# A two-layer diffusion transformer: output projection with latent tokens first, and norm and first up pair by halves of the tokens

## The chip, the cores and the metric

The kernel runs on one core of one Trainium2 chip. The metric is the device time of one execution, in microseconds (us). The core has five engines that work side by side, each with a queue that it follows in order: TensorE (PE, matrix products), VectorE (DVE), ScalarE (ACT), GpSimd (POOL) and SyncE (SP), which only issues loads and stores. They wait for each other by semaphores.

## The reference

Two layers over 512 latent and 256 context tokens of width 1024. Layer 0 mixes tokens by multi-head latent attention, layer 1 by a gated recurrence; each is followed by a SwiGLU feed-forward block of width 2816. The context stream is updated in layer 0 only. The change lies behind the two mixers:

```python
mod_l = jnp.split((jax.nn.silu(c) @ ada_w[i] + ada_b[i])[:, None, :], N_MOD, axis=-1)
mod_c = jnp.split((jax.nn.silu(c_ctx) @ ada_w[i] + ada_b[i])[None, None, :], N_MOD, axis=-1)
...
out_l = merge_heads(o_l) @ w_o
out_c = merge_heads(softmax_attend(q_c, k_c, v_c, scale)) @ w_o
...
x = x + mod_l[2] * o_l
x = x + mod_l[5] * swiglu(modulate(rms_norm(x, norm2_w[i]), mod_l[3], mod_l[4]),
                          ffn_w1[i], ffn_w3[i], ffn_w2[i])
if update_ctx:
    h_ctx = h_ctx + mod_c[2] * o_c
    h_ctx = h_ctx + mod_c[5] * swiglu(modulate(rms_norm(h_ctx, norm2_w[i]), mod_c[3], mod_c[4]),
                                      ffn_w1[i], ffn_w3[i], ffn_w2[i])
```

## The kernel before

**Products.** Activations lie transposed: 128 channels on the partitions, tokens along the free axis. Every fp32 operand is split in two parts, `hi` (a cast to a shorter format, on ScalarE) and `lo` (the rest, a subtraction). Each product is three matmuls, hi·hi, hi·lo and lo·hi (`mm3`, L97 to L99; `mm3m`, L108 to L110, the same for several outputs in turn). A weight block is 128x1024, 512 KB: `weight` loads it into one of four raw buffers (`wf`), ScalarE casts it (`wh`, L83) and GpSimd makes the low part (`wl`, L84), three buffers each. The loads of the modulation weights (`adaw`, in `ada`, L155; products L158, transposes L164) share the four raw buffers.

**Order.** A scheduler of the framework fixes the order of the instructions of each engine ahead of the run, out of the order in which the code issues them, their priorities and the dependences. All loads named here stand in SP's queue.

**Output projection of layer 0.** `w_o` has eight blocks n, one for each 128 output channels. For n = 0 to 2 the product over the 512 latent tokens is computed inside attention, where it fills TensorE's gaps, and stays in three accumulator banks. `mla_out` then goes over n = 0 to 7: the latent product where it is missing (24 matmuls of 128x512), the context product (24 of 128x256) with the same weight, and `residual`, which adds the gated result to x (L557) and the squares to `acc` for the norm. In the rows `oc` and `oa` are the attention results that the products read, `q` is one of five accumulator banks, `L` and `M` are three more.

**Norm.** `norm_rb` makes the reciprocal root of the mean square of each token: transposes of `acc` on TensorE (L205), a reduction on VectorE (L208), a power on GpSimd (L209), a diagonal on VectorE (L212, `dg`), and a product with ones that spreads it over the partitions (L215).

**First up pair.** `ffn` scales x by norm and modulation (L665 on VectorE, L667 on ScalarE) and splits it into operands `op` (L628, L629), for j = 0 to 3 and for two blocks of channels each, over all tokens. The pair needs the tokens as two halves b of hn = 384 (layer 0) or 256 (layer 1) tokens. `strassen_tokens` (L704 to L707, on GpSimd) then makes sums of the quarters for the other ten pairs, which use seven products in place of eight. `ffn_first` computes the first pair directly: for i = 0 and 1 it loads a block of W1 and of W3 and runs four products at once, W1 and W3 for both halves. These are 4 x 48 = 192 matmuls. `ffn_up` does the further pairs, with sums of raw weights (`sa`, `sb`, L611 to L615, on VectorE) and their own casts (`sh`, `sl`, L622, L623).

## Time and profile before

| | |
|---|---|
| time, median of three runs | 1845.55 us (1845.32 to 1850.65) |
| the profiled execution's own time | 1853.65 us |
| its span in the trace | 1851.9 us |
| busy: PE, DVE, ACT, POOL | 1755.5, 1016.3, 762.6, 760.6 us |
| mean granted TensorE clock | 0.982 |
| moved by DMA | 183.61 MB, 99 GB/s on average |

The span runs from the first to the last instruction of one profiled execution; the metric also holds what lies around it. The rows of a timeline give the start of an instruction in us from the span's start, how long it took, the engine, the source line, the operation, the tiles written and read, and in brackets how long the engine stood idle before it and what it waited for. Matmuls overlap each other, so what one of them costs in a dense stretch is the distance between two starts and not its own duration. "x2" is a run of two instructions, with the time of both. The granted clock is a share of TensorE's full 2.4 GHz; its other level is 1.2 GHz.

### The profile page before, as it was taken

The page shows a single profiled execution, that of the slowest core. Times are in us where ns is not written, and L with a number is a line of the kernel's source. Part 1 is how long each engine was busy: PE and PEld are TensorE (multiplying, and loading weights), DVE is VectorE, ACT ScalarE, POOL GpSimd, SP SyncE. Part 2 cuts the span into 40 slices and gives each one's busy share as a digit, 9 for nine tenths or more (in the row PEclk, how much of TensorE's full clock was granted, in tenths as well). Part 3 has the DMA queues.
Part 4 walks back from the last instruction along what each step waited for, and adds up shares of the span by engine and source line. Part 5 has one row for each costly group of instructions (what it writes and reads, how often), then busy time and mean ns, then how long its engine had stood idle before and what let it go on. Part 6 is the DMA issues. An engine that isn't in the chain of part 4 may idle for free. (4 is left out here: it accounts for less than half of the span.)

```text
span 1851.9 us, 33106 instructions
## 1 busy us (share of the span) xinstructions
PE 1755.5 (95%) x13708; PEld 1591.8 (86%) x13708; DVE 1016.3 (55%) x1646; ACT 762.6 (41%) x1467; POOL 760.6 (41%) x528
## 2 busy tenths in 40 slices
PE   4889999999899999999999999999998889999999
PEld 3878989788799999988887888888896779999888
DVE  5567887741754445432203666575745278888400
ACT  4355565532554344432213332423333255555411
POOL 2333342216566666643344554554643440000442
PEclk9999999999999999999999999999999989999999
DMA  7412032523222322254224121111115233333331
GB/s 268 137 39 73 25 116 98 170 74 122 103 86 97 104 96 103 81 168 136 86 71 148 60 69 47 61 55 58 58 35 191 94 137 103 103 115 103 108 118 49
DMA packets 55015, 183.61 MB, mean 99 GB/s; under 512 B 6224, under 2 KB 8528, under 8 KB 54864
## 3 DMA queue, kind: packets, MB, share of 16 engines
q1 hardware_dynamic: 53424, 173.62, 28.5%
q10 hardware_dynamic: 1440, 7.86, 1.2%
q8 instruction: 108, 1.77, 0.4%
q14 instruction: 43, 0.35, 0.1%
HBM read 171.50 MB, written 9.96 MB: 98 GB/s over the span
## 5 line engine op out<-in xcount | busy, mean ns | idle before, releaser
L84 POOL TENSOR_TENSOR wl<-wf,wh 128x1024 fp32r<-128x1024 f32 (+2 forms) x130 | 287.0, 2214 | 438.9 <-ACT wh L83 436.5
L83 ACT CAST wh<-wf 128x1024 fp32r<-128x1024 f32 (+2 forms) x130 | 122.9, 947 | 226.2 <-PE L L98 102.5
L97 PE MATMUL q<-op,sh 128*128 128x384 f32 (+1 forms) x640 | 197.3, 310 | 1.0 <-ACT sh L622 1.0
L98 PE MATMUL q<-op,sh 128*128 128x384 f32 (+1 forms) x640 | 197.6, 310 | 0.0
L99 PE MATMUL q<-op,sl 128*128 128x384 f32 (+1 forms) x640 | 194.9, 310 | 0.0
L97 PEld LDWEIGHTS q<-op,sh 128*128 128x128 f32 x640 | 120.3, 188 | 1.5 <-ACT sh L622 1.5
L98 PEld LDWEIGHTS q<-op,sh 128*128 128x128 f32 x640 | 120.3, 188 | 0.0
L99 PEld LDWEIGHTS q<-op,sl 128*128 128x128 f32 x640 | 119.5, 188 | 0.0
L623 POOL TENSOR_TENSOR sl<-wf,sh 128x1024 fp32r<-128x1024 f32 (+1 forms) x40 | 88.7, 2218 | 56.4 <-ACT sh L622 56.4
L98 PE MATMUL L<-op,sh 128*128 128x256 f32 (+1 forms) x360 | 110.4, 307 | 0.0
L99 PE MATMUL L<-op,sl 128*128 128x256 f32 (+1 forms) x360 | 110.3, 306 | 0.0
L97 PE MATMUL L<-op,sh 128*128 128x256 f32 (+1 forms) x360 | 110.3, 306 | 0.0
L1060 DVE TENSOR_TENSOR X<-X,T 128x512 f32<-128x512 f32 x96 | 78.1, 855 | 47.0 <-PE lv L985 45.9
L557 DVE SCALAR_TENSOR_TENSOR xl<-L,mod,xl 128x512 f32<-128x512 f32 x24 | 17.9, 750 | 153.8 <-PE L L99 149.8
L622 ACT CAST sh<-wf 128x1024 fp32r<-128x1024 f32 x80 | 66.7, 834 | 70.2 <-PE L L98 32.7
L98 PE MATMUL L<-f_lo,wh 128*128 128x512 f32 (+1 forms) x240 | 89.1, 371 | 0.0
L97 PE MATMUL L<-f_hi,wh 128*128 128x512 f32 (+1 forms) x240 | 89.0, 371 | 0.0
L99 PE MATMUL L<-f_hi,wl 128*128 128x512 f32 (+1 forms) x240 | 88.5, 369 | 0.0
L158 PE MATMUL L<-adaw,s 128*32 128x128 f32 x1216 | 57.1, 297 | 29.5 <-DMA adaw<-in_ADA 29.3
L975 POOL TENSOR_SCALAR km<-X 128x512 f32<-128x512 f32 x40 | 29.4, 737 | 125.5 <-DVE X L1060 76.4
L622 ACT CAST sh<-sb 128x1024 fp32r<-128x1024 f32 x40 | 42.0, 1050 | 88.5 <-PE q L98 46.6
L158 PEld LDWEIGHTS L<-adaw,s 128*32 128x32 f32 x1216 | 34.8, 116 | 46.1 <-DMA adaw<-in_ADA 17.2
(466 smaller groups left out, 5585.3 us busy)
## 6 DMA issues: line engine op xcount, KB each, us to landing
wf<-in_W SPq DMA_DIRECT2D x104, 512.0 KB, 3.5
adaw<-in_ADA SPq DMA_DIRECT2D x96, 512.0 KB, 4.4
wf<-in_HW SPq DMA_DIRECT2D x32, 512.0 KB, 3.5
wf<-in_W SPq DMA_DIRECT2D x24, 384.0 KB, 3.2
gd<-s SPq DMA_DIRECT2D x10, 768.0 KB, 3.5
g<-gd ACTq DMA_DIRECT2D x10, 768.0 KB, 4.7
wf<-in_W SPq DMA_DIRECT2D x16, 320.0 KB, 3.0
wf<-in_MWO SPq DMA_DIRECT2D x8, 512.0 KB, 4.1
```

The lines of the kernel that those rows point to most:

```text
L83: nc.scalar.copy(hi[:, :n], w[:, :n])
L84: nc.gpsimd.tensor_sub(lo[:, :n], w[:, :n], hi[:, :n].bitcast(F32))
L97: nc.tensor.matmul(out, lhsT=lh, rhs=rh, start=(new and i == 0), stop=False, skip_group_check=more)
L98: nc.tensor.matmul(out, lhsT=lh, rhs=rl, start=False, stop=False, skip_group_check=more)
L99: nc.tensor.matmul(out, lhsT=ll, rhs=rh, start=False, stop=(i == n - 1), skip_group_check=more)
L158: nc.tensor.matmul(rows_ps[32 * j:32 * j + 32, i * P:(i + 1) * P], lhsT=self.s32[:, k, :], rhs=w[:, k * P:(k + 1) * P], start=(k < 4), sto ...
L557: nc.vector.scalar_tensor_tensor(xk, po, gate[:, s:s + 1], xk, op0=ALU.mult, op1=ALU.add)
L622: nc.scalar.copy(hi[:, :n], s)
L623: (nc.vector if j in on_dve else nc.gpsimd).tensor_sub(lo[:, :n], s, hi[:, :n].bitcast(F32))
L975: nc.gpsimd.tensor_scalar(km.rearrange("p (m b r) -> p m b r", b=2, r=L), mix, 1.0, 0.0, op0=ALU.mult, op1=ALU.add)
L1060: nc.vector.tensor_tensor(v, v, t, op=ALU.mult)
```

## The change

**Projection.** `mla_out` computes all eight latent products first (n = 3 to 7 into the five `q` banks), then the eight context products, n = 7 first and then 0 to 6. The weights n = 0 to 6 are loaded and cast a second time for that, and their low parts are made on VectorE instead of GpSimd. The norm of the latent tokens is computed behind the third context product, that of the context tokens at the end.

**Norm and first pair by halves.** `ffn` is handed the finished norm, in both layers. Scaling and splitting run over the halves b outside and j inside. `ffn_first` goes through (b, i) as (0,0), (0,1), (1,1), (1,0), two products at once instead of four; the weights of i = 0 are loaded a second time for the last step.

The number of matmuls stays the same. In the queues there are 11 loads of 512 KB more (7 of `w_o`, 2 of W1 and W3 in each layer), as many casts on ScalarE, 7 subtractions more on VectorE, and 4 more on GpSimd.

```diff
-    def weight(self, name, idx, c0, c1, place=None):
+    def weight(self, name, idx, c0, c1, place=None, eng=None):
...
             nc.scalar.copy(hi[:, :n], w[:, :n])
-            nc.gpsimd.tensor_sub(lo[:, :n], w[:, :n], hi[:, :n].bitcast(F32))
+            (eng or nc.gpsimd).tensor_sub(lo[:, :n], w[:, :n], hi[:, :n].bitcast(F32))
...
     def mla_out(self, o, outs, x, ps, spool, acc):
+        gate = lambda n: self.mod[0][:, 16 + n, :]
+        bank = lambda: self.bank(ps)
         for n in range(KD):
-            w, po = outs[n] if n < len(outs) else (self.weight("MWO", (n,), 0, 1024), [])
-            po = po + self.proj_out(ps, self.out_terms(w, o), SEGS[len(po):])
-            self.residual(x, n, po, self.mod[0][:, 16 + n, :], SEGS, spool, acc)
+            w, po = outs[n] if n < len(outs) else (self.weight("MWO", (n,), 0, 1024), None)
+            po = po or self.proj_out(ps, self.out_terms(w, o), SEGS[:1], [bank()])
+            self.residual(x, n, po, gate(n), SEGS[:1], spool, acc)
+        rbs = []
+        for j, n in enumerate((KD - 1, *range(KD - 1))):
+            if j:
+                w = self.weight("MWO", (n,), 0, 1024, eng=nc.vector)
+            po = self.proj_out(ps, self.out_terms(w, o), SEGS[1:])
+            self.residual(x, n, po, gate(n), SEGS[1:], spool, acc, j)
+            if j == 2:
+                rbs += self.norm_rb(acc, SEGS[:1], spool, lambda i, c0, c1: bank()[:, :c1 - c0], bank)
+        return rbs + self.norm_rb(acc, SEGS[1:], spool, lambda i, c0, c1: bank()[:, :c1 - c0], bank)
...
-    def ffn(self, es, l, x, segs, acc, ps, spool=None, acc1=None):
+    def ffn(self, es, l, x, segs, rbs, ps, spool=None, acc1=None):
...
-            rbs = self.norm_rb(acc, segs, fs, lambda i, c0, c1: self.bank(ps)[:, :c1 - c0], lambda: self.bank(ps))
...
-            ys, los = [], []
-            for j in range(KP):
-                y = None
-                for i, k in enumerate((j, j + KP)):
-                    y = y or st()
...
-                    for (s, c0, c1), rb in zip(segs, rbs):
...
-                    for b in range(2):
...
-                        los.append(self.split(o[:, 0], o[:, 1], y[:, 2 * i + b, :], nc.vector))
+            ys, los = [st() for _ in range(KP)], []
+
+            for b in range(2):
+                parts = [(s, max(c0, b * hn), min(c1, b * hn + hn), rb, c0) for (s, c0, c1), rb in zip(segs, rbs)
+                         if max(c0, b * hn) < min(c1, b * hn + hn)]
+                for j, y in enumerate(ys):
+                    for i, k in enumerate((j, j + KP)):
+                        t = y[:, 2 * i + b, :]
+                        for s, c0, c1, rb, r0 in parts:
+                            tc = t[:, c0 - b * hn:c1 - b * hn]
...
+                            nc.scalar.activation(tc, tc, AF.Identity, bias=self.mod[l][:, 24 + k, s:s + 1])
                         o = ops[j][:, :, (0, 3, 1, 2)[2 * i + b], :]
+                        los.append(self.split(o[:, 0], o[:, 1], t, nc.vector))
...
     def ffn_first(self, l, p, hn, ops, fs, ps, st):
...
-        for i in range(2):
+        ws = {}
+        for b, i in ((0, 0), (0, 1), (1, 1), (1, 0)):
             outs = []
             for m in ("W1", "W3"):
-                wh, wl = self.weight(m, (l, 2 * p + i), 0, 1024)
-                for b in range(2):
-                    terms = [((wh[:, k * P:(k + 1) * P], wl[:, k * P:(k + 1) * P]), tuple(ops[j][:, q, t, :] for q in range(2)))
-                             for j in range(len(ops)) for k, t in ((j, 3 * b), (j + len(ops), 1 + b))]
-                    outs.append((self.up_bank(ps, hn), terms))
+                if b == 0 or i == 0:
+                    ws[m] = self.weight(m, (l, 2 * p + i), 0, 1024)
+                wh, wl = ws[m]
+                terms = [((wh[:, k * P:(k + 1) * P], wl[:, k * P:(k + 1) * P]), tuple(ops[j][:, q, t, :] for q in range(2)))
+                         for j in range(len(ops)) for k, t in ((j, 3 * b), (j + len(ops), 1 + b))]
+                outs.append((self.up_bank(ps, hn), terms))
             self.mm3m(outs)
...
             for n in range(5, KD):
                 out(n, SEGS[:1] if n < KD - 1 else HALF, ps)
+            with ExitStack() as es3:
+                bank = lambda: self.bank(ps)
+                rbs = self.norm_rb(acc, HALF, self.pool(es3, "n3b"), lambda i, c0, c1: bank()[:, :c1 - c0], bank)
...
             with ExitStack() as es2:
-                self.ffn(es2, 1, x, HALF, acc, ps)
+                self.ffn(es2, 1, x, HALF, rbs, ps)
```

How the order of the queues moves is seen at three places.

ScalarE, layer 0, end of attention, before: `pt_hi` is the attention weights' high part (L532), `oa` the high part of attention's result, `wh` a weight of the projection.

```order
L628 CAST oa<-ov 128x256
L532 CAST pt_hi<-tp_4652 128x2x128
L532 CAST pt_hi<-tp_4671 128x2x128
L628 CAST oa<-ov 128x256
L187 ACTIVATE acc<-xl 128x512
L190 ACTIVATE sq<-xl 128x512
L83 CAST wh<-wf 128x1024
L187 ACTIVATE acc<-xc 128x256
L83 CAST wh<-wf 128x1024
```

After, the same place:

```order
L641 CAST oa<-ov 128x256
L532 CAST pt_hi<-tp_4652 128x2x128
L83 CAST wh<-wf 128x1024 x3
L532 CAST pt_hi<-tp_4671 128x2x128
L641 CAST oa<-ov 128x256
L187 ACTIVATE acc<-xl 128x512
L190 ACTIVATE sq<-xl 128x512 x2
L83 CAST wh<-wf 128x1024
```

Three casts of projection weights have moved ahead of the last `pt_hi`; before, they followed the first residual sums. (Lines behind L560 have moved by 13 or 14: L628 is L641 now, L629 is L642, L665 is L679, L611 is L624.)

TensorE, layer 0, from the end of the projection to the first pair, before: `acc` holds the sums of squares, `dg` the diagonal of the norm, `adaw` the modulation weights, `op` the operands of the first pair.

```order
L99 MATMUL q<-oa,wl 128x256
L158 MATMUL M<-adaw,s_79 32x128 x13
L205 MATMUL q<-ident,acc 128x128 x4
L158 MATMUL M<-adaw,s_79 32x128 x18
L205 MATMUL q<-ident,acc 128x128 x2
L158 MATMUL M<-adaw,s_79 32x128
L164 MATMUL L<-ident,rows 128x128 x4
L158 MATMUL L<-adaw,s_79 32x128 x8
L215 MATMUL q<-dg,ones 128x512
L158 MATMUL L<-adaw,s_79 32x128 x8
L215 MATMUL q<-dg,ones 128x256
L158 MATMUL L<-adaw,s_79 32x128 x16
L108 MATMUL q<-op_5457,wh 128x384 x2
```

After, first the place of the latent norm, amid the context products:

```order
L99 MATMUL q<-oa,wl 128x256
L205 MATMUL q<-ident,acc 128x128 x4
L215 MATMUL q<-dg,ones 128x512
L97 MATMUL q<-oc,wh 128x256
```

And the end of the projection after the change:

```order
L99 MATMUL q<-oa,wl 128x256
L158 MATMUL L<-adaw,s_79 32x128 x32
L158 MATMUL M<-adaw,s_79 32x128 x8
L164 MATMUL L<-ident,rows 128x128 x4
L205 MATMUL q<-ident,acc 128x128 x2
L158 MATMUL M<-adaw,s_79 32x128 x24
L215 MATMUL q<-dg,ones 128x256
L108 MATMUL q<-op_5521,wh 128x384
```

The latent norm's transposes and its spreading product have moved up between context products, and follow each other directly, where modulation products stood between them before. In SP's queue the seven second loads of `w_o` stand directly ahead of the first pair's two weights and the eight `adaw` loads, and the two weights of i = 0 come again behind those of i = 1.

VectorE, layer 1, first pair, before: `op` are the operands (the numbers tell j apart), `s` the scaled tokens, `sa` and `sb` the raw weight sums of the second pair.

```order
L629 TENSOR_TENSOR op_14989<-s,op_14989 128x256
L665 SCALAR_TENSOR_TENSOR s<-xl,nsc_14980,q 128x256 x2
L611 TENSOR_TENSOR sa<-wf 128x512
L614 TENSOR_TENSOR sb<-wf 128x512
L629 TENSOR_TENSOR op_14989<-s,op_14989 128x256
L629 TENSOR_TENSOR op_14990<-s,op_14990 128x256
L665 SCALAR_TENSOR_TENSOR s<-xl,nsc_14980,q 128x256 x2
L612 TENSOR_TENSOR sa<-sa,wf 128x512
L629 TENSOR_TENSOR op_14990<-s,op_14990 128x256 x3
L629 TENSOR_TENSOR op_14991<-s,op_14991 128x256 x2
```

After, from the last scalings on:

```order
L679 SCALAR_TENSOR_TENSOR s<-xl,nsc_15074,q 128x256
L642 TENSOR_TENSOR op_15082<-s,op_15082 128x256
L679 SCALAR_TENSOR_TENSOR s<-xl,nsc_15074,q 128x256
L642 TENSOR_TENSOR op_15083<-s,op_15083 128x256 x2
L642 TENSOR_TENSOR op_15084<-s,op_15084 128x256 x2
L642 TENSOR_TENSOR op_15085<-s,op_15085 128x256 x2
L624 TENSOR_TENSOR sa<-wf 128x512
L627 TENSOR_TENSOR sb<-wf 128x512
L625 TENSOR_TENSOR sa<-sa,wf 128x512
L628 TENSOR_TENSOR sb<-wf,sa 128x512
```

Before, `sa` and `sb` stand between the splits, with nine of sixteen splits still to come; after, they come behind the last split.

## Rows read from the trace of the kernel before

**Rows 1.** The page, busy time (us, share of the span, instructions) of TensorE.
```profile
PE 1755.5 (95%) x13708; PEld 1591.8 (86%) x13708; DVE 1016.3 (55%) x1646; ACT 762.6 (41%) x1467; POOL 760.6 (41%) x528
```

**Rows 2.** Timeline of TensorE, end of attention and projection; columns start us, us, what.
```profile
407.55 0.41 PE L98 MATMUL L<-oa,wh 128*128 128x512 f32 x1
...
409.79 0.38 PE L97 MATMUL ov<-pt_hi,v_hi 128*128 128x256 f32 x1 [0.46 <-ACT pt_hi L532]
...
421.99 0.50 PE L99 MATMUL L<-oc,wl 128*128 128x512 f32 x1 [1.66 <-POOL wl L84]
```

**Rows 3.** Timeline of TensorE, layer 0, projection's end, first pair's start and end.
```profile
463.10 0.28 PE L99 MATMUL q<-oa,wl 128*128 128x256 f32 x1
...
474.41 0.65 PE L158 MATMUL L<-adaw,s 128*32 128x128 f32 x16 [2.02 <-DMA adaw<-in_ADA]
474.98 0.62 PE L108 MATMUL q<-op,wh 128*128 128x384 f32 x2
...
517.47 0.34 PE L110 MATMUL q<-op,wl 128*128 128x384 f32 x1
517.64 0.34 PE L99 MATMUL q<-op,sl 128*128 128x384 f32 x1
```

**Rows 4.** Windows; busy us of PE, PEld, DVE, ACT, POOL, then granted clock.
```profile
422.00:442.00 20.00, 20.00 (x110) 17.51 (x111) 2.47 (x4) 5.04 (x8) 15.55 (x11) 1.00 0.36 115
475.00:480.00 5.00, 4.72 (x22) 4.30 (x18) 3.04 (x5) 4.88 (x11) 3.49 (x3) 0.66 0.59 206
475.00:517.64 42.64, 38.32 (x204) 36.11 (x201) 30.56 (x39) 28.38 (x49) 29.67 (x20) 0.96 0.19 62
1493.10:1525.60 32.50, 28.24 (x220) 27.03 (x217) 27.15 (x41) 22.42 (x49) 20.30 (x18) 0.89 0.29 98
1503.00:1510.00 7.00, 5.55 (x26) 5.55 (x27) 7.00 (x13) 3.08 (x6) 4.83 (x6) 0.52 0.19 69
```

**Rows 5.** Timeline of TensorE, first up pair of layer 1.
```profile
1493.10 0.50 PE L108 MATMUL q<-op,wh 128*128 128x256 f32 x2
...
1504.45 0.58 PE L109 MATMUL M<-op,wh 128*128 128x256 f32 x1 [3.77 <-DVE op L629]
...
1525.50 0.28 PE L110 MATMUL q<-op,wl 128*128 128x256 f32 x1
1525.62 0.28 PE L99 MATMUL q<-op,sl 128*128 128x256 f32 x1
```

**Rows 6.** Timeline of ScalarE, a weight's cast in the projection.
```profile
418.13 1.04 ACT L83 CAST wh<-wf 128x1024 fp32r<-128x1024 f32 x1
```

**Rows 7.** The tile adaw, eight loads in layer 0, 425 to 476 us.
```profile
DMA to landing us min/median/max: 3.4/3.6/7.5
```

**Rows 8.** Timeline of VectorE, a low part of the shape 128x1024.
```profile
1521.24 1.21 DVE L623 TENSOR_TENSOR sl<-sa,sh 128x1024 fp32r<-128x1024 f32 x1
```

**Rows 9.** Timeline of all engines, the norm of layer 0.
```profile
464.99 0.69 DVE L208 TENSOR_REDUCE nr<-q 128x4 f32<-128x512 f32 x1
...
465.76 1.02 POOL L209 TENSOR_TENSOR nr<-nr,half 128x4 f32<-128x4 f32 x1 [6.59 <-DVE nr L208]
...
466.92 0.68 DVE L212 TENSOR_TENSOR dg<-ident,nr 128x512 f32<-128x512 f32 x1
```

**Rows 10.** Timeline of VectorE, layer 1, operands and weight sums.
```profile
1493.99 0.45 DVE L629 TENSOR_TENSOR op<-s,op 128x256 fp32r<-128x256 f32 x1
1494.36 0.86 DVE L665 SCALAR_TENSOR_TENSOR s<-xl,nsc,q 128x256 f32<-128x256 f32 x2
...
1499.74 2.67 DVE L611 TENSOR_TENSOR sa<-wf 128x512 f32<-128x512 f32 x1
1502.33 1.21 DVE L614 TENSOR_TENSOR sb<-wf 128x512 f32<-128x512 f32 x1
```

**Rows 11.** Groups of GpSimd by shape, 475 to 518 us: low parts.
```profile
L84 POOL TENSOR_TENSOR wl<-wf,wh 128x1024 fp32r<-128x1024 f32 x2 | 4.8, 2420 | 3.0 <-ACT wh L83 3.0
```

**Rows 12.** Timeline of GpSimd, layer 0, token operations.
```profile
500.68 2.00 POOL L706 TENSOR_TENSOR s<-s,T 128x384 f32<-128x384 f32 x1 [0.56 <-DVE op L629]
```

More of the change, by code (lines that the diff above doesn't have):

```diff
@@ L205, in norm_rb @@
                 nc.tensor.transpose(tp[:, t * P:(t + 1) * P], acc[:, c0 + t * P:c0 + (t + 1) * P], self.ident)
-            r = pool.tile([P, 2, LT], F32, tag=f"nr{i}", name="nr", bufs=1)
+            r = pool.tile([P, 2, LT], F32, tag=f"nr{c0}", name="nr", bufs=1)
             rs.append((r, t4))
@@ L296, in layer0 @@
                 acc = spool.tile([P, NT], F32, tag="acc", name="acc")
-                self.mla_out(o, outs, x, ps, spool, acc)
+                rbs = self.mla_out(o, outs, x, ps, spool, acc)
                 mla.close()
@@ L302, in layer0 @@
                 with ExitStack() as es2:
-                    self.ffn(es2, 0, x, SEGS, acc, ps, spool, acc1)
+                    self.ffn(es2, 0, x, SEGS, rbs, ps, spool, acc1)
                 self.dumpx("xf0", x)
@@ L549, in mla_attend, with residual @@
         return os, outs
-    def residual(self, x, k, pos, gate, segs, pool=None, acc=None):
+    def residual(self, x, k, pos, gate, segs, pool=None, acc=None, j=None):
         nc = self.nc
@@ L558, in residual @@
                 if acc is not None:
-                    self.sq_add(pool, acc, xk, s, k, c0, c1)
+                    self.sq_add(pool, acc, xk, s, k if j is None else j, c0, c1)
     def po(self, ps, n):
@@ L596, in mla_out @@
     def mla_out(self, o, outs, x, ps, spool, acc):
+        nc = self.nc
+        gate = lambda n: self.mod[0][:, 16 + n, :]
+        bank = lambda: self.bank(ps)
         for n in range(KD):
-            w, po = outs[n] if n < len(outs) else (self.weight("MWO", (n,), 0, 1024), [])
-            po = po + self.proj_out(ps, self.out_terms(w, o), SEGS[len(po):])
-            self.residual(x, n, po, self.mod[0][:, 16 + n, :], SEGS, spool, acc)
+            w, po = outs[n] if n < len(outs) else (self.weight("MWO", (n,), 0, 1024), None)
[10 more added lines that the diff above has]
+        return rbs + self.norm_rb(acc, SEGS[1:], spool, lambda i, c0, c1: bank()[:, :c1 - c0], bank)
     def strassen_weights(self, raw, w, fs, on_dve):
@@ L655, in ffn @@
             T1 = T1.rearrange("p a b c -> p (a b c)")[:, :KP * hn].rearrange("p (j c) -> p j c", j=KP)
-            ys, los = [], []
-            for j in range(KP):
-                y = None
-                for i, k in enumerate((j, j + KP)):
-                    y = y or st()
-                    y2 = y.rearrange("p a b -> p (a b)").rearrange("p (a b) -> p a b", a=2)
-                    t = y2[:, i]
-                    for (s, c0, c1), rb in zip(segs, rbs):
-                        with self.tc.issue_after(los[-LAG].ins) if len(los) >= LAG else nullcontext():
-                            nc.vector.scalar_tensor_tensor(t[:, c0:c1], x[s][:, k, c0 - SEGS[s][1]:c1 - SEGS[s][1]], sc[:, k, s:s + 1], rb,
-                                                           op0=ALU.mult, op1=ALU.mult)
-                        nc.scalar.activation(y2[:, i, c0:c1], t[:, c0:c1], AF.Identity, bias=self.mod[l][:, 24 + k, s:s + 1])
-                    for b in range(2):
+            ys, los = [st() for _ in range(KP)], []
[7 more added lines that the diff above has]
+                            tc = t[:, c0 - b * hn:c1 - b * hn]
+                            with self.tc.issue_after(los[-LAG].ins) if len(los) >= LAG else nullcontext():
+                                nc.vector.scalar_tensor_tensor(tc, x[s][:, k, c0 - SEGS[s][1]:c1 - SEGS[s][1]], sc[:, k, s:s + 1],
+                                                               rb[:, c0 - r0:c1 - r0], op0=ALU.mult, op1=ALU.mult)
+                            nc.scalar.activation(tc, tc, AF.Identity, bias=self.mod[l][:, 24 + k, s:s + 1])
                         o = ops[j][:, :, (0, 3, 1, 2)[2 * i + b], :]
-                        los.append(self.split(o[:, 0], o[:, 1], y[:, 2 * i + b, :], nc.vector))
-                ys.append(y)
+                        los.append(self.split(o[:, 0], o[:, 1], t, nc.vector))
             for j, y in enumerate(ys):
```

2 lines of the change are left out of this document (1 added, 1 removed).

## The prediction

> **What bounds the kernel now.** I read the page's busy shares first: TensorE is busy for 95% of the span [rows 1], so the change can move the time only where TensorE stands still or runs at half clock, or where it makes it do so. The change touches two short stretches, so I read the timeline of TensorE there next: in layer 0 from the end of attention over the output projection to the end of the first up pair (407 to 518 us), in layer 1 the first up pair (1493 to 1526 us). The reader is to see three things. In layer 0 the projection is dense but for one wait of 1.66 us for a weight's low part [rows 2]. Behind it TensorE has only the modulation (ADA) matmuls until 474.98, and waits for their loads, 2.02 us the last time [rows 3]. The first pair then takes from 474.98 to 517.64 with 4.3 us of it idle (42.64 less 38.32), and in layer 1 from 1493.10 to 1525.6 with 4.3 us idle (32.50 less 28.24) [rows 4]. The granted clock says what more is lost: 0.66 in 475 to 480 us and 0.52 in 1503 to 1510 us, between stretches at 1.00 [rows 4]. These are the two levels 2.4 and 1.2 GHz mixed.
>
> **Matmuls.** The order lists as many as before, of the same shapes. In a dense stretch a 128x384 matmul starts 0.17 us behind another (517.47 and 517.64; the rows' rounding hides some, I take 0.176), which makes the pair's 192 matmuls worth 33.8 us; at 128x256 (1525.50 and 1525.62, on average 0.119) they are worth 22.9 us [rows 3, 5]. What the pairs take beyond that is what there is to win: 42.64 less 33.8 less 0.7 (four matmuls of the second pair lie inside) is 8.1 us in layer 0, and 32.5 less 22.9 less 0.5 is 9.1 us in layer 1, of which about 1.0 is ADA work that stays.
>
> **Layer 0, up to the first pair.** ScalarE now casts three weights (1.04 us each [rows 6]) ahead of the last `pt_hi`, which the last attention product needs. The slot of the first is free when TensorE has used the old weight, about 407.9 (the row at 407.55 and its 0.41). 407.9, three casts, 0.4 for `pt_hi` give 411.4, where the product started at 409.79: 1.7 us late [rows 2]. But the low part of the fourth weight is then made 1.7 us earlier against its use, and the wait of 1.66 us at 421.99 goes [rows 2]. I cost the two together at nothing, with +1.7 as the bound if the second does not go.
>
> The second load of seven weights is 3.7 MB on SP's queue. It stands ahead of the first pair's weights and the ADA loads, but is spread over the context products, 24 matmuls of 0.12 us, 2.9 us for each weight. An `adaw` load of the same size lands in 3.4 us at the least and is issued while others fly, 7.5 us at the worst [rows 7]; four raw buffers cover that. The seven casts (1.04) and the seven subtractions, now on VectorE (1.21 us in the one row of this shape on that engine [rows 8]), each fit into 2.9 us and lie under the products.
>
> The latent norm moves between the context products, and in TensorE's order nothing stands between its transposes and the product that broadcasts the result. VectorE's reduction (0.69), GpSimd's power (1.02) and VectorE's diagonal (0.68) [rows 9] run in sequence, and a subtraction of the new kind (1.21) may stand in VectorE's queue ahead: 2.4 to 3.6 us of wait that was not there. I take 2.9. The projection's end: from 409.79 + 1.7 the same 53.4 us that led to 463.2 less 1.66, 2.9 of wait, and 1.4 for the norm's own matmuls, which stood among the ADA work before, give 467.5.
>
> What follows is paced by DMA. Only the first four `adaw` loads can be issued ahead, the others as TensorE frees buffers after the projection. Before, from 463.2 to 474.98, this took 11.8 us, ending in the 2.02 us wait [rows 3]. After, the same eight loads start 4.3 us later; the context norm lies in their shadow. I put the first pair's start at 479 (477 with faster landings, 481 with the four weight loads among them): 4 us later than 474.98.
>
> **Layer 0, first pair.** The first products need only the first half of the tokens, six of whose eight scalings are done during the context products, and whose operands are split while the ADA tail runs. I remove the split waits and keep one stretch at half clock like that at 475 to 480 (1.7 us, 5.00 x 0.34), because a wait again precedes the pair. 479 + 33.8 + 0.6 (ADA transposes) + 1.7 is 515.1, against 517.64 less the 0.7 of foreign work: **-1.8 us**. Against it, each of the two waits placed new (1.7 before the last attention product, 2.9 in the norm) may bring half clock at 1.4 to 1.7 us. The 2.02 us wait was followed by 0.66, but the 1.66 us wait by 1.00 [rows 2 to 4]. So the second more likely does, the first hardly: +1.5. Layer 0: **-0.3 us**, bounds -5 and +4.
>
> The Trainium skill ("TensorE: Matmul & The Clock Gate", HAM oscillation) tells of matmul loops that fall to half rate again and again behind their waits. By that rule each new wait costs a half-rate stretch, and layer 0 gives +1.4 instead of -0.3; the trace agrees for 2.02 us and differs for 1.66 us.
>
> **Layer 1.** Here the single costly event is the wait of 3.77 us at 1504.45, and half clock after it [rows 4, 5]. VectorE's queue shows why: the next pair's raw weight sums, L611 2.67 us and L614 behind it, stood ahead of the operand split [rows 10]. In the new order these sums come behind all sixteen splits. The price of the event: 3.77, and 3.4 us lost at half clock (7.00 x 0.48). In its place: one operand of a half costs VectorE 0.45 + 0.43 us (half of 0.86) [rows 10], but feeds six matmuls, 0.72 us; over eight operands TensorE is 1.3 us short. The second weight's cast and low part may cost another 0.5. So the pair starts as before at about 1493.3 and takes 22.9 + 1.0 + 1.8 = 25.7 us, ending at 1519.0 instead of 1525.1 (1525.6 less 0.5): -6.1. I take **-5.7 us**, because the clock may fall once in the dense stretch too; bounds -7 and -2.
>
> **Sum.** -0.3 - 5.7 = -6.0 us on the profiled span of 1851.9 (1853.65 with what lies around it, 8.1 above the median of 1845.55). Against the median: **1839.5 us**. A measurement can tell about 0.3% (5.5 us) from no change.
>
> **Rivals.**
> *Layer 0 gains too.* No new half clock, and the first pair starts at 477: layer 0 gives -4, layer 1 -6.1, together -10: 1835.5. For it speaks that the first half's operands are ready early; against it, that the `adaw` loads are tied to the projection's end, now later. 0.17.
>
> *The waits return.* Both new waits bring half clock (+3), the loads land late (481, +2), and layer 1 gives only half, since VectorE's splits run beside two more GpSimd subtractions of 2.42 us per layer [rows 11]: L611 took 2.67 us in such company, while its neighbour L614 took 1.21 [rows 10]. Layer 0 +2 to +3, layer 1 -3 to -4: about -1, 1844.5. 0.24. The Trainium skill ("SBUF — State Buffer", Who interferes with whom) has VectorE with two SBUF inputs and GpSimd hold a port pair in turn, one blocking the other for a whole instruction. By that, each of the two subtractions could block a split for its 2.4 us and layer 1 would give -1; the row of L611 agrees in size.
>
> *GpSimd becomes the bound (slower).* In layer 0 it is busy for 29.67 of the pair's 42.64 us in 20 instructions, in layer 1 for 20.30 in 18 [rows 4]. Two more subtractions make this 34.5 of about 36.1 and 25.1 of 25.7. It decides from the point where the sixteen token operations rise by 0.1 us each (from a mean of 1.25 in layer 0, that is 29.67 less four weight subtractions, by 16). A row of such an operation at 2.00 us is there [rows 12]. At a mean of 1.65 layer 0 ends 4.8 us late, and layer 1, in the same proportion, about 4.5: -6.0 + 9.3 is +3 to +7, say 1850.5. Against it: not all of the queue is due by the pair's end. 0.09.
>
> **How the numbers follow.** The forecast, -8.5 to -3.5, has 0.50. Faster by over 0.3% is the first rival and 0.31 of the forecast: 0.48. Within it the rest of the forecast, the second rival and the low end of the third: 0.44. Slower: 0.08. The likeliest case alone runs from 1837 to 1842. The range for 8 in 10 runs from 1833 (all of the first rival but its far end) to 1846.5, leaving out the third rival and the top of the second, some 0.17 in all.
>
> **What would show it.** In the changed trace: no wait of TensorE for a split above 1 us in layer 1's first pair, and its last L110 product near 1519 by the old time; a wait of 2.4 to 3.6 us before the product with `dg` amid the context products; the wait at 421.99 gone; the layer-0 pair starting about 4 us later than before and running in 36 us. The prediction is wrong if that pair starts beyond 481, if the clock of 1493 to 1520 stays below 0.85, or if TensorE waits for GpSimd's `wl` by more than 2 us.

## The result: slower, 1856.45 us

The changed kernel takes 1856.45 us in the median of 20 runs (1849.73 to 1862.03), the kernel before 1846.22 us in as many. The ratio is 1.0053, with a 95% interval of 1.0039 to 1.0066: 9.8 us slower. The forecast was 1839.5 us.

The two profiled executions hide this. The one of before was itself a long one (1853.65 us, 7.4 above its median), the one of after (1853.88 us, span 1851.4) is 2.6 below its own. So nothing is read from the spans below, only from stages. A second sign comes from the runs themselves, each of which lists its mean granted clock: 0.9854 on average for the kernel before (35 runs) and 0.9794 for the changed one (20 runs). One minus these shares, times spans of 1846 and 1854 us, is 27 and 38 us; the difference, 11 us, has the size of the slowdown. It is only a pointer, since half clock under an idle TensorE costs nothing, and a weak one: the two fastest kernels below, `proj_late` and `norm_cast_dve`, have 0.9829 and 0.9832, less than the kernel before.

TensorE's timeline in layer 0 after the change:

```profile
410.95 0.58 PE L97 MATMUL ov<-pt_hi,v_hi 128*128 128x256 f32 x1 [1.98 <-ACT pt_hi L532]
...
449.32 0.60 PE L205 MATMUL q<-ident,acc 128*128 128x128 f32 x4
453.95 2.07 PE L215 MATMUL q<-dg,ones 128*128 128x512 f32 x2 [4.03 <-DVE dg L212]
...
471.38 0.28 PE L99 MATMUL q<-oa,wl 128*128 128x256 f32 x1
...
482.37 0.53 PE L108 MATMUL q<-op,wh 128*128 128x384 f32 x1
...
517.27 0.34 PE L110 MATMUL q<-op,wl 128*128 128x384 f32 x1
...
520.07 0.62 PE L99 MATMUL q<-op,sl 128*128 128x384 f32 x1 [1.82 <-POOL sl L636]
...
528.40 0.44 PE L98 MATMUL q<-op,sh 128*128 128x384 f32 x1 [1.46 <-DVE op L642]
...
529.95 0.45 PE L98 MATMUL q<-op,sh 128*128 128x384 f32 x1 [0.76 <-DVE op L642]
...
555.36 0.34 PE L99 MATMUL M<-op,sl 128*128 128x384 f32 x1
```

The last attention product waits 1.98 us for `pt_hi` (0.46 before) and the stall for a low part at 421.99 is gone [rows 2]. The norm's product waits 4.03 us. The projection ends at 471.38 instead of 463.10 and the first pair starts at 482.37 instead of 474.98, but its last product stands at 517.27, where it stood at 517.47 [rows 3]: the pair has become 7.6 us shorter. Then come three waits that were not there, 1.82, 1.46 and 0.76 us, all in the second pair. The row at 555.36 is that pair's last L99 product on the operands; in the trace of before it is this one:

```profile
546.96 0.34 PE L99 MATMUL L<-op,sl 128*128 128x384 f32 x1
```

The norm's chain, on all engines:

```profile
449.96 0.69 DVE L208 TENSOR_REDUCE nr<-q 128x4 f32<-128x512 f32 x1
...
450.57 1.22 DVE L84 TENSOR_TENSOR wl<-wf,wh 128x1024 fp32r<-128x1024 f32 x1
450.73 1.93 POOL L209 TENSOR_TENSOR nr<-nr,half 128x4 f32<-128x4 f32 x1 [1.30 <-DVE nr L208]
...
452.64 0.72 POOL L194 TENSOR_TENSOR acc<-acc,sq 128x256 f32<-128x256 f32 x1
452.69 1.21 DVE L212 TENSOR_TENSOR dg<-ident,nr 128x512 f32<-128x512 f32 x1 [0.91 <-POOL nr L209]
```

Windows after (busy us of PE, PEld, DVE, ACT, POOL, granted clock, DMA share, GB/s):

```profile
411.00:422.00 11.00, 11.00 (x44) 9.12 (x45) 3.78 (x6) 2.57 (x5) 6.34 (x5) 0.85 0.77 251
450.00:460.00 10.00, 6.04 (x27) 5.01 (x28) 6.23 (x10) 4.01 (x8) 2.62 (x2) 0.66 0.29 102
484.00:518.00 34.00, 33.38 (x191) 32.31 (x189) 22.81 (x24) 16.57 (x32) 32.16 (x21) 1.00 0.28 91
518.00:535.00 17.00, 12.95 (x54) 12.07 (x53) 15.96 (x13) 12.74 (x17) 8.59 (x4) 0.80 0.19 63
```

Around the wait of 1.98 us the clock is at 0.85 over 11 us, around the norm wait at 0.66 over 10 us. GpSimd is busy for 32.16 of 34 us in the stretch of the first pair, where the whole of the longer pair took 29.67 us of it before [rows 4]; the second pair's waits follow, with a clock of 0.80. Two of the three waits are for operands that VectorE splits. Its groups by shape, 500 to 535 us (in all us, mean ns), first after the change, then before:

```profile
L642 DVE TENSOR_TENSOR op<-s,op 128x1152 fp32r<-128x1152 f32 x4 | 9.1, 2314 | 3.3 <-ACT op L641 3.3
L642 DVE TENSOR_TENSOR op<-T,op 128x384 fp32r<-128x384 f32 x4 | 7.5, 1924 | 0.0
```

```profile
L629 DVE TENSOR_TENSOR op<-s,op 128x1152 fp32r<-128x1152 f32 x3 | 4.0, 1352 | 3.1 <-ACT op L628 3.1
L629 DVE TENSOR_TENSOR op<-T,op 128x384 fp32r<-128x384 f32 x4 | 2.3, 574 | 7.0 <-ACT op L628 7.0
```

Each split has become 1 to 1.4 us longer. They also start late. All engines but TensorE, after the change:

```profile
512.38 4.23 POOL L719 TENSOR_TENSOR s<-s 128x384 f32<-128x384 f32 x2
...
513.67 0.86 ACT L741 COPY s<-q 128x384 f32<-128x384 f32 x2 [4.28 <-DVE op L642]
...
516.51 1.06 ACT L635 CAST sh<-wf 128x1024 fp32r<-128x1024 f32 x1
...
517.65 2.37 POOL L636 TENSOR_TENSOR sl<-wf,sh 128x1024 fp32r<-128x1024 f32 x1 [1.04 <-PE q L110]
...
519.04 3.47 DVE L642 TENSOR_TENSOR op<-s,op 128x1152 fp32r<-128x1152 f32 x2 [3.30 <-ACT op L641]
```

GpSimd's last token sums (L719) end at 516.61, 0.7 us ahead of the first pair's last product. Before, they ended at 504.65, 12.8 us ahead of it:

```profile
502.65 2.00 POOL L707 TENSOR_TENSOR s<-s 128x384 f32<-128x384 f32 x2
```

The splits of these sums follow them. The wait of 1.82 us for `sl` has another way. GpSimd stood idle for 1.04 us before this low part; the cast `sh` that it needs ends at 517.57, and the profile names the first pair's last L110 product, which ends at 517.61, as the last that it waited for. The cast stands in ScalarE's queue behind copies of the first pair's banks (L741), and the first of these waited 4.28 us for a split of VectorE.

Layer 1, TensorE:

```profile
1506.98 0.38 PE L109 MATMUL L<-op,wh 128*128 128x256 f32 x1 [1.00 <-DVE op L642]
...
1518.29 0.38 PE L97 MATMUL q<-op,sh 128*128 128x256 f32 x1 [1.93 <-ACT s L741]
...
1519.54 0.39 PE L99 MATMUL q<-op,sl 128*128 128x256 f32 x1 [0.76 <-DVE sl L636]
...
1528.43 0.39 PE L97 MATMUL q<-op,sh 128*128 128x256 f32 x1 [1.43 <-ACT sh L635]
```

The wait of 3.77 us [rows 5] is gone as forecast. In its place stand 1.00 us in the first pair, and 1.93, 0.76 and 1.43 us in the second.

### The profile page after: what moved, and what is told of

Same layout as the page of the kernel before. It is cut to its first block, busy times and chain, and to the rows that moved or that the text cites. A ratio compares the mean times of both kernels' runs of the same rounds, so it can differ in the third digit from the quotient of the medians.

```text
span 1851.4 us, 33170 instructions
## 1 busy us (share of the span) xinstructions
PE 1753.7 (95%) x13708; PEld 1588.8 (86%) x13708; DVE 1037.0 (56%) x1661; ACT 773.7 (42%) x1486; POOL 780.2 (42%) x532
## 5 line engine op out<-in xcount | busy, mean ns | idle before, releaser
L84 POOL TENSOR_TENSOR wl<-wf,wh 128x1024 fp32r<-128x1024 f32 (+2 forms) x134 | 297.9, 2229 | 465.3 <-ACT wh L83 431.8
L83 ACT CAST wh<-wf 128x1024 fp32r<-128x1024 f32 (+2 forms) x141 | 134.0, 955 | 251.5 <-PE L L98 94.2
L99 PE MATMUL q<-op,sl 128*128 128x384 f32 (+1 forms) x640 | 195.7, 311 | 2.6 <-POOL sl L636 1.8
L99 PEld LDWEIGHTS q<-op,sl 128*128 128x128 f32 x640 | 120.6, 190 | 3.1 <-POOL sl L636 2.1
L99 PE MATMUL L<-op,sl 128*128 128x256 f32 (+1 forms) x280 | 85.4, 305 | 0.0
L97 PE MATMUL L<-op,sh 128*128 128x256 f32 (+1 forms) x280 | 85.4, 306 | 0.0
L98 PE MATMUL L<-op,sh 128*128 128x256 f32 (+1 forms) x280 | 85.2, 305 | 0.0
L98 PE MATMUL L<-gs,wh 128*128 128x512 f32 x202 | 79.6, 394 | 3.2 <-DVE gs L642 3.1
L97 PE MATMUL L<-gs,wh 128*128 128x512 f32 x202 | 79.5, 393 | 2.6 <-ACT gs L641 2.6
L97 PE MATMUL L<-f_hi,wh 128*128 128x512 f32 (+1 forms) x232 | 79.5, 343 | 0.0
L98 PE MATMUL L<-f_lo,wh 128*128 128x512 f32 (+1 forms) x232 | 79.4, 342 | 0.0
L99 PE MATMUL L<-gs,wl 128*128 128x512 f32 x202 | 79.2, 392 | 0.0
L99 PE MATMUL L<-f_hi,wl 128*128 128x512 f32 (+1 forms) x232 | 78.9, 340 | 0.0
```

The lines of the kernel that those rows point to most:

```text
L83: nc.scalar.copy(hi[:, :n], w[:, :n])
L84: (eng or nc.gpsimd).tensor_sub(lo[:, :n], w[:, :n], hi[:, :n].bitcast(F32))
L97: nc.tensor.matmul(out, lhsT=lh, rhs=rh, start=(new and i == 0), stop=False, skip_group_check=more)
L98: nc.tensor.matmul(out, lhsT=lh, rhs=rl, start=False, stop=False, skip_group_check=more)
L99: nc.tensor.matmul(out, lhsT=ll, rhs=rh, start=False, stop=(i == n - 1), skip_group_check=more)
```

## Experiments

All ratios are to the kernel before, run on the same chips. "Stage 0" is the time from the last attention-score product (L518) to the last L99 product of layer 0's second pair, "stage 1" that from the end of layer 1's projection to the same product of its second pair. They are read from the one trace of each kernel, so a stretch at half clock more or less (1.7 us for one like that at 475 to 480 us before [rows 4]) is in them. Each edit makes the scheduler order the whole program anew: the edit of `norm_late` lies in layer 0, yet in layer 1 4 products of the second pair stand ahead of the first pair's end and not 23 as in the changed kernel. So an edit is never quite alone, in "stage 1" least of all.

```
kernel            ratio   95% interval      stage 0: projection | to pair | pair 1 | pair 2 | sum     stage 1
before            1                                     63.2       11.9      42.5     29.5    147.0    62.6
changed           1.0053  1.0039 to 1.0066              70.5       11.0      34.9     38.1    154.5    63.4
after_again       1.0057  1.0040 to 1.0074              71.3       11.8      34.2     38.7    155.9    63.4
proj_only         1.0011  0.9995 to 1.0028              70.9        9.0      39.7     32.4    152.0    60.3
pair0_only        1.0008  0.9988 to 1.0028              61.8       11.6      43.6     32.5    149.6    65.5
pair1_only        0.9988  0.9973 to 1.0003              61.7       10.5      44.5     29.1    145.8    66.7
norm_late         1.0012  0.9994 to 1.0030              62.7       11.0      37.7     35.6    147.0    64.5
cast_late         1.0047  1.0028 to 1.0066              69.7       11.1      34.9     38.1    153.7    64.2
norm_cast         1.0027  1.0012 to 1.0041              63.1       12.0      36.4     36.8    148.3    63.3
lo_dve            1.0016  0.9998 to 1.0034              70.9       11.8      33.8     36.0    152.4    60.2
norm_cast_dve     0.9980  0.9967 to 0.9993              65.3       11.6      37.3     33.1    147.3    60.2
norm_cast_first   0.9989  0.9971 to 1.0007              65.3       10.7      39.2     32.3    147.5    62.4
pair1_dve         0.9982  0.9964 to 1.0000              64.2       12.1      44.0     29.1    149.4    64.0
proj_late         0.9969  0.9947 to 0.9990              63.1        9.0      37.9     32.3    142.2    60.3
```

After the result I held two theories. A: the norm wait and the half clock behind it cost the projection about 7 us, and what the first pair wins is given back in the second, whose operands are late because of GpSimd's two further subtractions in each layer. B, the rival: the costs come from the second load of the weights, the modulation work in one block, or VectorE's own queue.

**The changed kernel again** (`after_again`, no edit).

> The changed kernel once more, on the chip of the three runs that follow, for a second trace and for its granted clock. Expected: 9 to 11 us slower than before; a mean granted clock of about 0.979, where the runs of the kernel before have 0.985 on average; again a norm wait of about 4 us, and waits of 3 to 5 us in layer 0's second pair.

1.0057, 1858.07 us, clock 0.9795; the norm wait is 4.04 us, and the second pair's waits 1.83, 1.45 and 0.75 us. Slowdown and waits belong to the kernel and not to one execution.

**The parts alone.** `proj_only` keeps the new `mla_out` and calls `ffn` and `ffn_first` of before; `pair0_only` and `pair1_only` have the old `mla_out` with the norm behind it, and the new `ffn` in one layer. In all three the norm is handed to `ffn`, as after the change.

```diff
# proj_only (ffn_o, ffn_first_o: the functions before the change)
-                    self.ffn(es2, 0, x, SEGS, rbs, ps, spool, acc1)
+                    self.ffn_o(es2, 0, x, SEGS, rbs, ps, spool, acc1)
...
-                self.ffn(es2, 1, x, HALF, rbs, ps)
+                self.ffn_o(es2, 1, x, HALF, rbs, ps)
```

> Only the new output projection of layer 0 (latent products first, second load, latent norm amid the context products); scaling, splits and first pair of both layers as before. Theory A (the projection itself costs): the trace after shows the norm wait of 4.03 us and a half-clock stretch behind it, and the first pair starting 6.5 us late against the start of attention's end; so 5 to 8 us slower than before, and the pair's waits for splits (2.3 us in layer 0) as before. Theory B (the cost arises only because the pair by halves follows): within 2 us of before.

> Projection as before, norm behind it; halves and the new order of the first pair in layer 0 alone, layer 1 as before. Theory A (what the first pair wins, the second pair gives back, since its operands hang on GpSimd's and VectorE's queues): the first pair ends 5 to 6 us earlier after its start than before, the second pair waits 3 to 4 us with half clock behind, and the sum is 0 to 3 us slower. Theory B (the second pair's waits come from the late start of the pair): they are gone, and the sum is 4 to 6 us faster.

> Layer 0 wholly as before, halves and new order of the first pair in layer 1 alone. Theory A (given back in the second pair): the wait of 3.8 us for a split is gone, the second pair waits some 4.6 us in all, the sum within 2 us of before. Theory B, the prediction's: 4 to 6 us faster.

`proj_only` is 1.0011, less than theory A said; but its projection takes 70.9 us, with a norm wait of 4.04 us, as A said. Its first pair waits for splits as theory A said, 1.24 and 1.36 us. Stage 1, whose code is the old one but for the earlier norm, was 2.3 us shorter in this trace: in the new order of the queues the wait of 3.77 us is one of 2.25 us, and the clock of 1503 to 1510 us is 0.76 there and not 0.52.

`pair0_only` is 1.0008: its second pair takes 32.5 us against 29.5, the giving back of A in small. But its first pair takes 43.6 us, 1.1 more than before, where theory A had 5 to 6 less: it waits 2.08 us for a low part of GpSimd, 0.96 us for a cast and four times up to 0.5 us for splits. So the 7.6 us that the changed kernel's first pair won are not earned by the halves alone; with the norm behind the projection they are not there.

`pair1_only` is 0.9988: neither the forecast's 4 to 6 us nor a clear nothing. In its trace the wait of 3.77 us has become three for splits in the first pair, 1.45, 1.33 and 1.86 us.

The three do not add up to the change: +2.0, +1.5 and -2.2 us make +1.3, not +9.8. In their traces stage 0 does add up (+4.9 and +2.5 against +7.5). The intervals of the four ratios together allow a gap of some 6 us, and it is 8.5: the spread of the runs alone does not make it, and why the parts cost more together than singly stays open.

**The norm late.** The transposes, reduction and power stay behind the third context product; diagonal and spreading product are issued behind the fifth.

```diff
             if j == 2:
-                rbs += self.norm_rb(acc, SEGS[:1], spool, lambda i, c0, c1: bank()[:, :c1 - c0], bank)
+                rs = self.norm_root(acc, SEGS[:1], spool, bank)
+            if j == 4:
+                rbs += self.norm_spread(rs, SEGS[:1], spool, lambda i, c0, c1: bank()[:, :c1 - c0])
```

> The changed kernel with the latent norm's diagonal and spreading product issued behind the fifth context product instead of the third, its transposes where they were. Theory A (the norm wait and the half clock behind it cost 4.0 and 3.4 us): that wait is gone, and the kernel is 5 to 8 us faster than the changed one, so within 5 us of the kernel before. Theory B (the first pair is paced by the modulation loads and by its operands, so the projection's end does not matter): 0 to 2 us faster than the changed one.

1.0012, 4.1 thousandths below the changed kernel: 7.6 us back, give or take 4 by the two intervals, as theory A has it. TensorE's timeline and window there (L209 and L225 are the transposes and the product):

```profile
443.07 0.60 PE L209 MATMUL q<-ident,acc 128*128 128x128 f32 x4
...
449.26 1.02 PE L225 MATMUL q<-dg,ones 128*128 128x512 f32 x2
```

```profile
430.00:460.00 30.00, 29.92 (x251) 28.26 (x249) 17.85 (x25) 15.12 (x26) 13.37 (x10) 1.00 0.41 125
```

No wait stands before the product, and the clock is 1.00 throughout. The projection takes 62.7 us instead of 70.5. Of these 7.8 us 1.7 are the half clock behind the wait for `pt_hi` (11.00 x 0.15 in the window above), which this trace does not have; the rest, about 6 us, is the wait and its half clock, the price of the norm's place. The second load of seven weights costs nothing that shows. The first pair takes 37.7 us here and not 34.9, for it waits 2.09 us for a low part of GpSimd.

**The casts late.** The three casts are held behind the last `pt_hi`.

```diff
-            nc.scalar.copy(hi[:, :n], w[:, :n])
+            with self.tc.issue_after(after.ins) if after else nullcontext():
+                nc.scalar.copy(hi[:, :n], w[:, :n])
...
-            w, po = outs[n] if n < len(outs) else (self.weight("MWO", (n,), 0, 1024), None)
+            w, po = outs[n] if n < len(outs) else (self.weight("MWO", (n,), 0, 1024, after=self.last_pt), None)
```

> The changed kernel, with the three casts of projection weights held behind the last high part of attention (pt_hi); nothing else. Theory A (the wait of 1.98 us for pt_hi costs little, since the same casts save the stall of 1.66 us): within 2 us of the changed kernel. Theory B (this wait is one of those that bring half clock): the mean granted clock rises by 0.001 or more and the kernel is 2 to 4 us faster than the changed one.

1855.72 us beside 1858.07 us on the same chip, clock 0.9793 beside 0.9795. The wait for `pt_hi` falls from 1.96 to 0.46 us, and one of 1.59 us for a low part comes back. Theory A holds within what six runs can tell: the two cancel.

**Both**, and then the second load's low parts on VectorE:

```diff
# norm_cast: the two edits above; norm_cast_dve also
-                    ws[m] = self.weight(m, (l, 2 * p + i), 0, 1024)
+                    ws[m] = self.weight(m, (l, 2 * p + i), 0, 1024, eng=nc.vector if b else None)
```

> The changed kernel with the latent norm's product behind the fifth context product and the three casts behind the last pt_hi. Theory A (half clock behind the new waits is what made the change slow): the mean granted clock comes back to 0.983 or more, and the kernel is within 2 us of before, or faster. Theory B (the half clock comes from the modulation tail and the second pair): the clock stays at 0.981 or below, and 3 us or more slower than before remain.

> As the run before it, and the low parts of the first pair's second weight load (two in each layer) made on VectorE in place of GpSimd. Theory A (GpSimd's queue makes the second pair's operands late): the second pair's waits fall from 3 to 5 us to below 2 us in layer 0, and the kernel is 3 to 6 us faster than the run before it. Theory B (VectorE's own queue or ScalarE's copies make them late): the waits stay or move to VectorE, within 2 us.

`norm_cast` is 1.0027, between the two theories: the clock is back at 0.9833, but 5 us of slowdown remain. `norm_cast_dve` is 0.9980, 9.1 us faster than `norm_cast` beside it, more than theory A had, and faster than the kernel before, with a clock that is no higher (0.9832). Its second pair still waits 0.47, 1.08 and 0.74 us, 2.3 us in all, and its first pair 2.39 us for a low part of GpSimd and 0.63 us for one of VectorE.

**Only the low parts** (`lo_dve`): the changed kernel with the last edit alone.

> The changed kernel with one edit: the low parts of the first pair's second weight load on VectorE in place of GpSimd, in both layers. Theory A (GpSimd's two further subtractions per layer make the second pair's operands late): layer 0's waits for sl and op behind the first pair (1.82, 1.46, 0.76 us) go with their half clock, and 5 to 9 us come back, whatever the norm wait does; the norm wait of 4.0 us and 6.8 us of half clock behind it stay. Theory B (the gain came only together with the norm and cast edits): less than 3 us.

1.0016, 3.7 thousandths or 6.8 us below the changed kernel, again give or take 4. TensorE's waits from 480 to 545 us there (us in total, times, longest):

```profile
PE q L99 <- POOL sl L636: 2.6, 2, 1.8
PE M L97 <- ACT s L770: 1.0, 1, 1.0
```

The two waits for `op` (1.46 and 0.76 us) are gone, as A said; the one of 1.8 us for `sl` is not, so that one does not come from the two subtractions. All engines but TensorE there:

```profile
504.43 4.09 POOL L719 TENSOR_TENSOR s<-s 128x384 f32<-128x384 f32 x2
...
507.67 0.86 ACT L741 COPY s<-q 128x384 f32<-128x384 f32 x2 [3.44 <-DVE op L642]
...
512.81 2.35 POOL L636 TENSOR_TENSOR sl<-wf,sh 128x1024 fp32r<-128x1024 f32 x1 [4.30 <-ACT sh L635]
...
513.56 7.90 DVE L642 TENSOR_TENSOR op<-T,op 128x384 fp32r<-128x384 f32 x4 [1.14 <-ACT op L641]
```

The token sums end at 508.52, 4.2 us ahead of the first pair's last product (512.67), where the changed kernel has 0.7. The four splits of 128x384 take 7.90 us, as long as the 7.5 us in the changed kernel, and no wait follows: they start 0.9 us behind the pair's last product and not 5.2 (522.42). So the two subtractions made TensorE wait for `op` by the late start of these splits, not by their length. GpSimd is idle for 4.30 us before `sl`, again for ScalarE's cast.

In layer 1 the 1.93, 0.76 and 1.43 us became one of 2.94 us for the new low part itself, now late on VectorE, and stage 1 falls by 3.2 us. The norm wait stays at 4.04 us. The two single edits give back 7.6 and 6.8 us, 14.4 together; `norm_cast_dve`, which has both and the late casts, is 7.3 thousandths or 13.5 us below the changed kernel. They add up.

**No second load** (`norm_cast_first`): `ffn_first` of before on the operands by halves, with the norm and the casts late.

> The norm late and the casts late as in norm_cast, with the first pair's products in the old order (i outside, four banks, no second load of W1 and W3) on the operands by halves. Theory A (the second load's work on GpSimd is the cost): no wait for sl or op above 1 us in the second pair, as fast as norm_cast_dve within 4 us, 3 us or more faster than norm_cast. Theory B (the order by halves itself earns the time, the second load only has to be cheap): the first pair waits for its second half's operands by 3 us or more, and it is slower than norm_cast_dve by 4 us or more.

0.9989, 1.7 us slower than `norm_cast_dve` by the ratios, with intervals that overlap. The first pair waits 1.22, 0.15 and 1.37 us for operands in layer 0, 2.7 us in all, and 1.37 us for a low part of GpSimd, the second for nothing above 0.8 us. All three of theory A's lines are met, the last by 3.8 thousandths (7.0 us) against `norm_cast`; B's two are not. Without the second load its cost is gone, and the new order of the products shows no gain over the old one.

**Layer 1 alone, low parts on VectorE** (`pair1_dve`: `pair1_only` with the edit of `lo_dve`).

> Layer 0 wholly as before; layer 1 by halves in the new order, with the second load's low parts on VectorE. Theory A: layer 1 from the projection's end to the first tenth of its up products takes about 60 us, where it took 62.6 before, and the kernel is 2 to 5 us faster than before. Theory B (no gain in layer 1 from halves): within 2 us of before.

0.9982: 3.3 us faster, at the edge of its interval, though its one trace shows 64.0 us in stage 1 and not 60 (it was one of the long executions, clock 0.976). Open.

**The new projection, repaired, with the old pairs** (`proj_late`).

> Only the new output projection, with the norm's product late and the three casts late; scaling, splits and first pair of both layers as before. Theory A (of the projection's cost nothing is left once the norm does not stall TensorE): within 2 us of before, mean granted clock 0.984 or more. Theory B (the second load of the weights or the modulation tail costs by itself): 3 us or more slower than before.

0.9969 (0.9947 to 0.9990), the lowest ratio of all, though its interval overlaps that of `norm_cast_dve`: 5.7 us faster than the kernel before, where both theories had no gain. Its mean clock is 0.9829, below the 0.984 of theory A. TensorE's waits from 480 to 545 us in its trace:

```profile
PE L L110 <- DVE op L655: 1.7, 2, 0.9
PE q L100 <- POOL sl L649: 0.7, 1, 0.7
```

The pair's waits for operands, 0.66, 0.69 and 0.96 us before, are 1.7 us in all here, and the way from projection to pair is 9.0 us instead of 11.9: in this kernel's order a quarter of the modulation products stands behind the pair's start. So the early norm and the old pairs do at least as well as the halves; whether they do better these runs can't tell.

## Why the prediction was wrong

**Projection.** The mechanism was named and the term mis-sized: the wait in the norm was put at 2.9 us (2.4 to 3.6) and measured 4.03, because GpSimd's power took 1.93 us and VectorE's diagonal 1.21, not 1.02 and 0.68 [rows 9]. In the rows above the power runs while VectorE makes a low part (450.57, 1.22 us), the diagonal while GpSimd adds squares (452.64, 0.72 us). The subtraction that I feared ahead in VectorE's queue was not there: it came behind the reduction. Half clock was given 1.5 us as a chance; the window at 0.66 is 3.4 us lost, a part of it under the wait, and a stretch at half clock stood there in all five traces that have the norm in this place. Together 7.6 us by `norm_late` (about 6 in the traces alone), where I had 4.4. The Trainium skill ("SBUF — State Buffer", Who interferes with whom) says that VectorE with two inputs in SBUF and GpSimd hold their shared ports in turn. The two stretched operations agree in size (0.91 and 0.53 us longer, beside partners that had 1.06 and 0.67 us still to run); no run here took one of the partners away alone.

**Casts.** Right: 1.7 us late was forecast, and a wait of 1.98 us in place of 0.46 came; the 1.66 us went.

**From the projection to the pair.** Right in length (11.0 us, forecast 11.5), late by the projection's error: the pair starts at 482.37 (481.45 if the time of before is counted on from the last attention-score product), and a start beyond 481 was one of the prediction's own signs of being wrong. Its other two did not come (clock of 1.00 from 1493 to 1520 us, no wait for `wl` above 0.37 us in either first pair); none of the three looked at the second pair.

**First pair of layer 0.** Right in the main: 34.9 us, forecast 36.1; no wait for a split. The stretch at half clock of 1.7 us that I kept did not come (clock 1.00). What made it short was the early norm as much as the halves (`pair0_only` above).

**Where the sum ended.** This is the step that failed: the sum stopped at the end of the first pair, as if what follows would move with it, and so put the second pair's waits at nothing. The second pair of layer 0 takes 38.1 us instead of 29.5. Both pairs together take 73.0 us where they took 72.0: what the first won, the second lost, and more. `proj_only`, with the old pairs, shows the same in small: 39.7 and 32.4 us, 72.1 together. The third rival had the place (GpSimd's queue, two subtractions more) and got 0.09. It let the result hang on the sixteen token operations becoming 0.1 us slower each. What the traces show is the end of the queue: the last token sums come 0.7 us ahead of the pair's end and not 12.8, partly for the two subtractions (four low parts `wl` in the stretch of the pair instead of two, 10.0 us instead of 4.8), partly because the pair is 7.6 us shorter (in `lo_dve` they come 4.2 us ahead of it, so 3.5 of the 12.1 us are the subtractions'). VectorE's splits, ScalarE's copies and casts stand behind them, and TensorE behind those. In `lo_dve`, without the two subtractions on GpSimd, both pairs together take 69.8 us; the waits for `op` are gone, the wait of 1.82 us for `sl` and its half clock stay.

**Layer 1.** The wait of 3.77 us went, as forecast, and came back in the second pair. The terms inside the first pair held: its waits for splits are 1.3 us in all, the shortage that I had. Its last product stands at 1526.13 instead of 1519, because 23 products of the second pair (2.7 us), their two waits (2.69 us) and the half clock behind these (1.7 us, 7.84 x 0.22 in the window below) lie ahead of it; without these it would stand at 1519.0. The window, and the timeline of all engines, after the change:

```profile
1518.29:1526.13 7.84, 7.08 (x45) 6.88 (x46) 6.66 (x6) 6.88 (x13) 5.56 (x5) 0.78 0.39 134
```

```profile
1514.18 2.83 POOL L84 TENSOR_TENSOR wl<-wf,wh 128x1024 fp32r<-128x1024 f32 x1
...
1514.69 3.14 DVE L642 TENSOR_TENSOR op<-s,op 128x768 fp32r<-128x768 f32 x1
...
1517.86 0.37 ACT L741 COPY s<-q 128x256 f32<-128x256 f32 x1 [2.63 <-DVE op L642]
```

GpSimd makes a low part of the second load (2.83 us), and VectorE's split of 128x768, which took 1.22 us on average in the stretch from 1493 to 1526 us before, takes 3.14 us beside it:

```profile
L629 DVE TENSOR_TENSOR op<-s,op 128x768 fp32r<-128x768 f32 x4 | 4.8, 1220 | 1.5 <-ACT op L628 1.5
```

It ends 0.82 us behind GpSimd's (1517.83 and 1517.01). This is what the rule of the Trainium skill named above would make of it, one of the two blocking the other for a whole instruction, and the prediction gave it a price in its second rival. ScalarE's copy of the first pair's banks (L741) is queued behind that split, and TensorE waits for the bank: 1.93 us at 1518.29. In `lo_dve`, which takes the low parts from GpSimd, no wait for this copy is left, though one of 2.94 us for a low part has come in its place. So the forecast of -5.7 us failed by the same omission as in layer 0, the second pair's waits; stage 1 is +0.8 us in the traces.

**Sum.** Put right, the forecast's terms read: the norm's place +7.6 us, GpSimd's low parts +6.8 us (both by single edits, each give or take 4), the remainder about -4 us (`norm_cast_dve` against before: -2.0 thousandths, -3.7 us). This remainder is smaller than the -6.0 that I had for the whole, and `proj_late` has as much without halves: that the pair by halves earns anything is not shown by these runs. How the remainder, and the gain of `lo_dve`, divide over the two layers stays open.

## What to carry to other kernels

Follow a sum past the stretch that is changed, until each engine's queue has caught up: a stage that becomes shorter leaves less cover for the work that prepares the next one, and additional work on an engine that was at 29.67 of 42.64 us is not hidden when the stretch shrinks to 35; it can hit through engines whose work stands behind it. A short dependent chain over three engines (reduction, power, diagonal) placed amid dense products needs its consumer issued late enough, here two products of 2.9 us further, or it stalls them and lowers the clock for the products behind it. Where runs scatter by 0.3%, single edits whose gains add up tell more than two traces. The mean granted clock of all runs does not rank kernels: that of the fastest here (0.9829) is below that of the kernel before (0.9854), and `norm_cast`, with 0.9833, is 5 us slower than before.

## What was not expected of the hardware

A wait of about 2 us did not decide alone whether the clock fell: the one of 1.96 to 1.98 us for `pt_hi` was followed by half clock in two of the five traces that have it, the one of 4.03 us in the norm in five of five. The spacing of 128x384 matmuls in the dense up products differed between executions at a granted clock of 1.00: layer 0's second pair took 29.5 us in the profiled execution of before and 29.1 us in those of `pair1_only` and `pair1_dve`, which have the old pairs there, 1.3% of that stretch, for which no view gives a reason.
